# RWKV pairs: three engines' instructions held in the order of the source, projections fed in stated numbers, weight loads issued five blocks ahead

## The chip, the core and the metric

The kernel runs on one core of a Trainium2 chip. The time is the device time of one execution, in microseconds. Five engines work beside each other, each through its own queue and in that queue's order: TensorE (PE; PEld is its weight load), VectorE (DVE), ScalarE (ACT), GpSimd (POOL) and SyncE (SP), the last of which here only issues DMAs. An instruction that waits on another engine's result holds up what stands behind it on its own.

## What is computed

A decoder block for 512 tokens of width 2048: RWKV-7 time mixing and windowed attention beside each other, both read from one projection of the normed input, merged by two sigmoid gates, then a gated convolutional FFN. The change lies in the RWKV part and in the projections that run beside it:

```python
h = rms_norm(x, norm1_g[l])
z = h @ w_in[l]                      # r, k, v, LoRA inputs, attention, gates
zs = token_shift(z[..., :RW_SHIFT_COLS], rw_mu[l])
...
def step(state, inp):                # 512 steps, 16 heads of 64
    r_t, k_t, v_t, w_t, ka_t, kb_t = inp
    sa = jnp.einsum('bhvk,bhk->bhv', state, ka_t)
    state = (state * w_t[:, :, None, :] + sa[..., None] * kb_t[:, :, None, :]
             + v_t[..., None] * k_t[:, :, None, :])
    y = jnp.einsum('bhvk,bhk->bhv', state, r_t)
    return state, y
...
y = ((y - mu) * lax.rsqrt(var + GN_EPS)).reshape(B, S, RW_DIM)
out = (y + bonus.reshape(B, S, RW_DIM)) * g.astype(f32)
```

## The kernel before

**Projections.** A tile of z is 128 channels by 512 tokens and is summed over 2048 inputs in 16 steps of 128. Weights and input are float32, each split into a high part and a remainder, and each step is three matmuls of 128x512: high by high, high by remainder, remainder by high (L255, L256, L257). So a tile is 48 matmuls. Its weights come in four blocks of four steps: a DMA of 256 KB into a tile `raw` (SP's queue), the high part `whi` copied by ScalarE (L238), the remainder `wlo` subtracted by VectorE (L239), and twelve matmuls. There are four buffers each of raw, whi and wlo.

**Pairs.** The 16 heads are worked in eight pairs, a pair being 128 channels. The recurrence is turned into chunks of 64 tokens, eight of them. `early(p)` makes a pair's rows: the k, r and v tiles with their token shift (`zpad` on ScalarE, then `kz`, `rz`, `vz` on VectorE, L536 and L537), k's norm (`rsqrt_small`, thirteen small steps on `rq` tiles, then a trip through DRAM that spreads it over rows), the decay (`lw`, two scans `Ei`, two exponentials into `Et` and `Ei`), and the bonus `bon`. `late(p)` makes the products of a chunk: grams `OW` and `AM` of `BKK` and `BAR`; a triangular inverse that is doubled from blocks of one to blocks of 64; the decayed keys `KD` and `KO`; and the chain.

**Levels.** The loop over `LEVELS[1:]` has five rounds. Each makes a first product `AI` by X (L773, L774: 16 short matmuls on float16 halves), sums and masks it on VectorE (L776, L790), splits it into `IW` (L791, L792), makes a second product `BT` by IW, sums that, writes it into `BX` and into X (L794 to L798), and turns X on TensorE (L802) into the next round's `BT` (four copies, L806 on VectorE and L808 on ScalarE). Every round waits for the one before.

**Chain.** The eight chunks follow each other: G from the state SS (L814, L816), U from BX and G (L820, a copy to `UU`), the next SS from KD and U (L827, L828). `final(p)` then adds up the outputs, norms them (square, `ssy`, thirteen `rq` steps, `yd`), turns them back, and multiplies by the gate's LoRA.

**Order.** The program issues late(p), early(p+1), final(p) and three gate tiles for each pair. A scheduler orders each engine's instructions anew: by its own view of what is ready, with program order as priority. Only what goes through `pin` (`tc.keep_in_program_order`) keeps its place: some matmuls (L625, L719, L820) and the splits that ask for it. So in each pair the 288 matmuls of six projections (k, r, v of the next pair and three gates) are laid by the scheduler between the pair's own short work. The output's splits `rhi`, `rlo` and the gates that are left follow the pairs.

Of the kernel before, what the change touches and what calls it, by code (L numbers as in the profile page):

```python
# [18 lines left out]
P = 128  # L19
S = 512  # L20
# [109 lines left out]
def block_kernel(ctx: ExitStack, tc: tile.TileContext, d: Dims, a: dict, out: bass.AP):  # L130
# [66 lines left out]
    def free(ins):  # L197
        return ins

# [76 lines left out]
    if True:  # L276
# [243 lines left out]
        with ExitStack() as pr:  # L520
# [4 lines left out]
            blk = pr.enter_context(tc.tile_pool(name="blk_ps", bufs=3, space=PSUM, reuse_waits="tile"))  # L525
            chn = pr.enter_context(tc.tile_pool(name="chn_ps", bufs=2, space=PSUM, reuse_waits="tile"))
# [95 lines left out]
            def heads_mm(dst, l, r, start, stop):  # L622
                for h, (lo, hi) in reversed(list(enumerate(HV))):
                    w = l[lo:hi] if l.shape[-1] == C else l[lo:hi, lo:hi]
                    pin(pe.matmul(dst[lo:hi], w, r[lo:hi], start=start, stop=stop, skip_group_check=True))  # L625

            def bulk_mm(dst, l, r):
                ps = bulk()
                for n in reversed(range(NCH)):
                    heads_mm(r3(ps)[:, n], l(n), r(n), True, True)  # L630
                act.activation(dst, r3(ps), AF.Copy)

            def early(p):
                wl = lp.tile([P, 2 + NG, P], F32, name="wl", tag="wl", bufs=2)
                sync.dma_start(wl, a["lora"][p].rearrange("p (k c) -> p k c", c=P))
                w2a2 = lora_parts(wl, 0)

                acc = ztile(d.c_k + p * P)
                kz = wtile("kz")
                shifted(acc, PR["mu"] + NP + p, kz, 0)  # L640
                kk = wtile("kk")
                dve.tensor_scalar(kk, kz, col("k_k", p), None, op0=ALU.mult)
                sq = wtile("lg")
                act.activation(sq, kk, AF.Square)
                ps = bulk()
                head_stats(ps, sq)
                rs = rsqrt_small(wk, ps[:, 0 : 2 * NT], None, None, mx=1e-24)
                rb = head_rows(wk, bulk(), rs, "lg")
                dve.tensor_tensor(kk, kk, rb, op=ALU.mult)


                ps = bulk()
                lora(ps, w2a2, (0,), 0)
                lg = wtile("lw")
                act.activation(lg, ps, AF.Tanh, scale=0.5)
                dve.tensor_scalar(lg, lg, 1.0, None, op0=ALU.add)
                Ei = wtile("Ei")
                for hs in (slice(0, S // 2), slice(S // 2, S)):
                    dve.tensor_tensor_scan(Ei[:, hs], going, lg[:, hs], 0.0, op0=ALU.mult, op1=ALU.add)
                act.activation(Et[:, :, 1:], r3(Ei), AF.Exp, scale=-0.5 * SQE)  # L660
                act.activation(Ei, Ei, AF.Exp, scale=0.5 * SQE)

                ps = bulk()
                lora(ps, w2a2, (1,), 0)
                ta = wtile("lw")
                act.activation(ta, ps, AF.Tanh, scale=0.5, bias=half[:, 0, p : p + 1])

                acc = ztile(d.c_r + p * P)
                rz = wtile("rz")
                shifted(acc, PR["mu"] + p, rz, 1)  # L670
                acc = ztile(d.c_v + p * P)
                vz = wtile("vz", 2)
                shifted(acc, PR["mu"] + 2 * NP + p, vz, 0)

                k2 = wtile("k2")
                dve.tensor_scalar(k2, ta, half[:, 1, p : p + 1], half[:, 2, p : p + 1], op0=ALU.mult, op1=ALU.add)
                dve.tensor_tensor(k2, k2, kz, op=ALU.mult)
                dve.tensor_scalar(ta, ta, 0.5, 0.5, op0=ALU.mult, op1=ALU.add)
                kb = kz
                dve.tensor_tensor(kb, kk, ta, op=ALU.mult)  # L680
                rk = wtile("lw")
                dve.scalar_tensor_tensor(rk, rz, col("r_k", p), k2, op0=ALU.mult, op1=ALU.mult)
                ps = bulk()
                pe.matmul(ps, K["bo"], rk, start=True, stop=True)
                bon = wtile("bon", 2)
                dve.tensor_tensor(bon, vz, ps, op=ALU.mult)
                act.activation(bon, bon, AF.Identity, bias=col("gn_b", p))
                return wl, Ei, kk, kb, k2, rz, vz, bon

            def late(p, st):  # L690
                wl, Ei, kk, kb, k2, rz, vz, bon = st
                Eex, Ein = Et[:, :, 0:C], Et[:, :, 1:]
                kb3, k23, Ei3, kk3, rz3, vz3 = (r3(x) for x in (kb, k2, Ei, kk, rz, vz))
                dve.tensor_tensor(BKK[:, :, 0:C], kb3, Ei3, op=ALU.mult)
                dve.tensor_tensor(BKK[:, :, C:P], k23, Ei3, op=ALU.mult)
                for h, hs in enumerate(slice(*x) for x in HV):
                    dve.scalar_tensor_tensor(BAR[hs, :, 1 + h], kk3[hs], -1.0, Eex[hs], op0=ALU.mult, op1=ALU.mult)
# [765 lines left out]
```

## Time and profile before

| what | value |
|---|---|
| three runs | 2847.71, 2839.99, 2846.57 us; median 2846.57 us |
| profiled execution | 2842.14 us, its span 2839.8 us |
| granted TensorE clock, mean | 0.997 |
| RWKV pairs, first gram to the last pair's end | 332.4 to 1100.8 us |
| a steady pair (630.5 to 729.3) | 98.8 us |

Times below are from the profiled execution. A row of a group names line, engine, operation, output and inputs, shape and count, then busy time in us, the mean of one in ns, and the idle time of the engine just ahead with what ended it. A row of a window gives the busy time of each engine within it.

### The profile page before, as it was taken

Reading aid. Unit: us, or ns where it says so; the run is one execution under the profiler, and the core shown is the slowest. Engines: PE = TensorE matmul, PEld = TensorE weight load, DVE = VectorE, ACT = ScalarE, POOL = GpSimd, SP = SyncE. Lnnn points to the kernel's source line nnn. Section 1 sums busy time; section 2 is a strip of 40 time slices with the busy share of each in tenths; the row PEclk is TensorE's granted clock in tenths of the full one; section 3 lists DMA queues with packets and bytes.
Section 4 is the critical chain, followed back from the end, with each engine's and each line's share of the span. In section 5 each row is a group of like instructions: output and inputs, shape, how many; then the busy total and the mean of one; then the engine's idle time right before and its main releaser. Section 6 shows DMA issues by size and latency. Waiting matters only on the chain.

```text
span 2839.8 us, 48133 instructions
## 1 busy us (share of the span) xinstructions
PE 2772.6 (98%) x18722; PEld 2413.2 (85%) x18722; DVE 1975.7 (70%) x3312; ACT 1289.0 (45%) x2075; POOL 230.8 (8%) x307
## 2 busy tenths in 40 slices
PE   7999999999999999999999999999999999999999
PEld 6888777777777777788888999999999999788887
DVE  5566677778777774455668777777777778655555
ACT  5345344334433433322465555555555555444444
POOL 0101000000000001011000101010101110000000
PEclk9999999999999999999999999999999999999999
DMA  6865676676667668888777789888988897877775
GB/s 190 232 155 152 174 181 166 159 179 162 164 152 177 164 173 240 241 245 275 245 260 200 220 237 245 225 226 232 244 229 224 231 241 227 313 242 241 257 257 189
DMA packets 223860, 608.06 MB, mean 214 GB/s; under 512 B 24576, under 2 KB 44688, under 8 KB 222608
## 3 DMA queue, kind: packets, MB, share of 16 engines
q1 hardware_dynamic: 156096, 432.49, 47.4%
q0 software_dynamic: 36832, 134.24, 24.6%
q10 hardware_dynamic: 30704, 38.27, 3.9%
q8 instruction: 146, 2.39, 0.3%
q14 instruction: 82, 0.67, 0.1%
HBM read 554.23 MB, written 174.40 MB: 257 GB/s over the span
## 4 chain that ended last, share of the span: by engine, by line
PE 86%; DVE 8%; DMA 2%; issue 1%; ACT 1%; ACTq 0%; SPq 0%; DVEq 0%
PE X L1164 18%; PE X L1031 11%; PE acc L255 9%; PE acc L257 9%; PE acc L256 9%; PE Y L1031 9%; PE Y L1164 8%; PE Z L1164 4%; PE bulk L625 1%; PE bulk L773 1%; DMA raw<-in_w_z_dram 1%; PE mi L508 1%; DMA raw<-in_w_dn_dram 1%; DVE BT L741 1%; PE bulk L802 1%
## 5 line engine op out<-in xcount | busy, mean ns | idle before, releaser
L257 PE MATMUL acc<-xhi,wlo 128*128 128x512 f32 x1120 | 450.3, 402 | 6.8 <-DVE wlo L239 6.8
L255 PE MATMUL acc<-xhi,whi 128*128 128x512 f32 x1120 | 450.1, 402 | 2.4 <-ACT whi L238 2.4
L256 PE MATMUL acc<-xlo,whi 128*128 128x512 f32 x1120 | 449.1, 401 | 0.0
L238 ACT ACTIVATE whi<-raw 128x512 fp32r<-128x512 f32 x352 | 220.7, 630 | 466.7 <-PE acc L256 353.3
L1024 DVE TENSOR_TENSOR wlo<-raw,whi 128x1024 fp32r<-128x1024 f32 x210 | 257.1, 1225 | 205.9 <-ACT whi L1023 204.3
L239 DVE TENSOR_TENSOR wlo<-raw,whi 128x512 fp32r<-128x512 f32 x352 | 240.3, 688 | 183.2 <-ACT whi L238 177.3
L1023 ACT ACTIVATE whi<-raw 128x1024 fp32r<-128x1024 f32 x210 | 222.6, 1060 | 291.0 <-PE X L1031 154.2
L1164 PE MATMUL X<-b,whi 128*128 128x256 f32 x1472 | 269.2, 283 | 2.3 <-DVE u L1184 0.9
L1147 DVE TENSOR_TENSOR wlo<-raw,whi 128x1024 fp32r<-128x1024 f32 x176 | 215.1, 1223 | 76.8 <-ACT whi L1146 76.5
L1164 PE MATMUL X<-t,whi 128*128 128x256 f32 x1408 | 259.1, 284 | 8.8 <-DVE u L1184 8.3
L1164 PE MATMUL Y<-t,whi 128*128 128x256 f32 x1408 | 257.1, 283 | 0.0
L257 PEld LDWEIGHTS acc<-xhi,wlo 128*128 128x128 f32 x1120 | 211.6, 189 | 46.4 <-DVE wlo L239 10.7
L255 PEld LDWEIGHTS acc<-xhi,whi 128*128 128x128 f32 x1120 | 211.4, 189 | 40.2 <-ACT whi L238 2.8
L256 PEld LDWEIGHTS acc<-xlo,whi 128*128 128x128 f32 x1120 | 211.8, 189 | 36.0
L1146 ACT ACTIVATE whi<-a 128x1024 fp32r<-128x1024 f32 x132 | 139.4, 1056 | 214.7 <-DVE a L1140 213.3
L1164 PEld LDWEIGHTS X<-b,whi 128*128 128x128 f32 x1472 | 229.5, 192 | 3.1 <-issue 2.4
L1164 PEld LDWEIGHTS X<-t,whi 128*128 128x128 f32 x1408 | 221.0, 193 | 9.3 <-DVE u L1184 5.7
L1164 PEld LDWEIGHTS Y<-t,whi 128*128 128x128 f32 x1408 | 219.6, 192 | 0.0
L1164 PE MATMUL X<-b,wlo 128*128 128x256 f32 x736 | 208.4, 283 | 2.1 <-DVE wlo L1147 2.1
L1147 DVE TENSOR_TENSOR wlo<-a,whi 128x1024 fp32r<-128x1024 f32 x132 | 161.7, 1226 | 67.4 <-ACT whi L1146 66.7
L1164 PE MATMUL X<-t,wlo 128*128 128x256 f32 x704 | 200.1, 284 | 0.0
L1164 PE MATMUL Y<-t,wlo 128*128 128x256 f32 x704 | 199.2, 283 | 0.0
(680 smaller groups left out, 5870.3 us busy)
## 6 DMA issues: line engine op xcount, KB each, us to landing
raw<-in_w_up_dram SPq DMA_DIRECT2D x180, 512.0 KB
raw<-in_w_z_dram SPq DMA_DIRECT2D x288, 256.0 KB
s_dn<-in_w_dn_dram POOLq DMA_DIRECT2D x88, 512.0 KB, 6.5
raw<-in_w_up_dram POOLq DMA_DIRECT2D x88, 512.0 KB, 8.3
raw<-s_dn SPq DMA_DIRECT2D x88, 512.0 KB
raw<-in_w_dn_dram SPq DMA_DIRECT2D x66, 512.0 KB
a<-in_w_up_dram SPq DMA_DIRECT2D x48, 512.0 KB
s_dn<-in_w_dn_dram SPq DMA_DIRECT2D x44, 512.0 KB
```

The source lines that it names most:

```text
L238: pin(act.activation(hi, raw, AF.Copy))
L239: pin(dve.tensor_tensor(lo, raw, hi.bitcast(F32), op=ALU.subtract))
L255: pe.matmul(acc, whi[:, j], xhi[:, k], start=first, stop=False)
L256: pe.matmul(acc, whi[:, j], xlo[:, k], start=False, stop=False)
L257: pe.matmul(acc, wlo[:, j], xhi[:, k], start=False, stop=last)
L508: pe.matmul(ps[:, h], pT[:, kb, h], vt[:, n - 1 + kb, g * HD : (g + 1) * HD], start=kb == kbs[0], stop=kb == kbs[-1])
L1023: act.activation(whi, wr, AF.Copy)
L1024: dve.tensor_tensor(wlo, wr, whi.bitcast(F32), op=ALU.subtract)
L1031: pe.matmul(dst, l[:, q, ts], r[:, es], start=fst and j == 0, stop=lst and j == 2, skip_group_check=True)
L1146: pin(act.activation(hi, t, AF.Copy))
L1147: pin(dve.tensor_tensor(lo, t, hi.bitcast(F32), op=ALU.subtract))
L1164: pin(pe.matmul(ps, l[:, k], r[:, k], start=start and k + i == 0, stop=last and i == 2, skip_group_check=True))
```

## The change

Every instruction that TensorE, VectorE or ScalarE gets in the pairs goes through a wrapper that pins it, so that on each engine the program's order is kept (all these instructions carry the wrapper's line, L207). DMAs are not pinned.

```diff
+    class Held:
+        def __init__(self, engine):
+            self.engine = engine
+        def __getattr__(self, name):
+            f = getattr(self.engine, name)
+            return f if name.startswith("dma") else lambda *args, **kw: pin(f(*args, **kw))
...
-            blk = pr.enter_context(tc.tile_pool(name="blk_ps", bufs=3, space=PSUM, reuse_waits="tile"))
-            chn = pr.enter_context(tc.tile_pool(name="chn_ps", bufs=2, space=PSUM, reuse_waits="tile"))
+            blk = pr.enter_context(tc.tile_pool(name="blk_ps", bufs=4, space=PSUM, reuse_waits="tile"))
+            chn = pr.enter_context(tc.tile_pool(name="chn_ps", bufs=1, space=PSUM, reuse_waits="tile"))
```

The projections become a stream of jobs. `feed(n)` issues the next n of its matmuls. Ahead of block n, loads up to block n+4 are issued and splits up to block n+2; the number of buffers stays four.

```diff
+            class Stream:
+                AHEAD, LOADS = 2, 5
...
+                def ready(self, n):
+                    while self.loaded < min(n + self.LOADS, len(self.blocks)):
...
+                        wp["last"] = sync.dma_start(raw.rearrange("p (k c) -> p k c", c=P), b[0])
...
+                    self.parts(n)
+                def parts(self, n):
+                    while self.parted < min(n + self.AHEAD + 1, self.loaded):
...
+                        split(hi, lo, b[1])
...
+                def feed(self, n):
+                    self.split = False
+                    while n and self.jobs:
+                        if next(self.jobs[0], True):
+                            self.jobs.pop(0)
+                        else:
+                            n -= 1
```

`early` and `late` are cut into steps (classes `Early`, `Pair`) which the loop over pairs calls one by one. The sum of a product's two halves, one reduce on VectorE before (L776), is a copy on ScalarE and an add on VectorE; BX is written by ScalarE except in the last round.

```diff
-                    dve.reduce_sum(t, p4.rearrange("p n e c -> p n c e"), axis=AX.X)
+                    act.activation(t, p4[:, :, 1], AF.Copy)
+                    dve.tensor_tensor(t, t, p4[:, :, 0], op=ALU.add)
...
-            st = early(0)
             for p in range(NP):
-                lt = late(p, st)
-                if p + 1 < NP:
-                    st = early(p + 1)
-                final(p, lt)
-                for _ in range(GATES_PER_PAIR * NK // 16):
-                    emit_gate()
+                own = nxt.jobs() if nxt else []
+                for job in [add_gate] + own[:2] + [add_gate] + own[2:] + [add_gate] * (1 if own else 4):
+                    job()
+                do = Pair(st)
+                st.dense_r()
+                if gone:
+                    gone.output_norms()
+                feed(13)
+                g = do.gram(0)
...
+                feed(15)
+                for m in LEVELS[1:]:
...
+                    do.first_out(p4, m)
+                    if i == 1:
+                        do.start_rest()
+                        if gone:
+                            gone.gated()
+                    if i == 2:
+                        do.decayed()
+                    if nxt and i == 3:
+                        nxt.norms()
...
+                    feed((20, 17, 17, 15, 15)[i - 1])
+                    p4 = do.second(m)
...
+                    do.second_out(p4, m)
+                    if i == 1 and nxt:
+                        nxt.k_rows()
+                    if i == 2:
+                        do.centred()
+                    if i == 3:
+                        do.keys_out(pk)
...
+                    feed((11, 12, 10, 10, 12)[i - 1])
+                    if i < 5:
+                        tp = do.turned()
+                along = iter(nxt.along() if nxt else ())
+                for _ in do.chain():
+                    if not stream.split:
+                        step = next(along, None)
+                        if step:
+                            step()
+                    feed(3)
...
+                do.outputs()
+                feed(5)
+                gone, st = do, nxt
+                nxt = Early(p + 2) if p + 2 < NP else None
+            gone.output_norms()
+            gone.scaled()
+            feed(30)
+            gone.back()
+            gone.back_out()
+            feed(12)
+            gone.gate()
+            gone.gated()
+            while gates:
+                add_gate()
+            feed(10 ** 6)
```

The numbers of one pair are 13, 12, 11, 17, 10, 15 (together 78) ahead of the rounds, 84 and 55 in them, 22 times 3 in the chain, and 5: 288, six projections. All gates that are left are issued straight behind the pairs, and the output's splits come after them.

Three places of the orders, before and after. First ScalarE in the rounds, second pair. Before, the copies of the decayed keys stand ahead of the rounds (`lg` is the square of the next pair's k):

```order
L238 ACTIVATE whi<-raw 128x512 x2
L762 ACTIVATE KD<-bulk 64x4x64
L763 ACTIVATE KO<-bulk 64x256
...
L536 ACTIVATE zpad_2830<-acc,par 128x512
L238 ACTIVATE whi<-raw 128x512
L631 ACTIVATE KV<-bulk 128x512
L644 ACTIVATE lg<-kk 128x512
L631 ACTIVATE GV<-bulk 128x512
L238 ACTIVATE whi<-raw 128x512
L794 ACTIVATE BX<-half__4790 64x8x16x2
L797 ACTIVATE XIW<-half__4790 128x128x2
L808 ACTIVATE BT<-bulk 64x8x64 x2
```

After, in the third and fourth round:

```order
L207 ACTIVATE half__5171<-bulk 128x8x32
L207 ACTIVATE XIW<-half__5171 128x32x8
L207 ACTIVATE BX<-half__5171 64x8x4x8 x2
L207 ACTIVATE KD<-bulk 64x4x64
L207 ACTIVATE KO<-bulk 64x256
...
L207 ACTIVATE whi<-raw 128x512
L207 ACTIVATE BT<-bulk 64x8x64 x2
L207 ACTIVATE half__5243<-bulk 128x8x32
```

KD and KO alternate four times each in both. They moved from ahead of the first round to the place between the third round's X and the fourth round's BT.

Second, VectorE between two pairs. Before, a split of the running projection stands among the small steps of the output's norm:

```order
L846 TENSOR_REDUCE ssy<-gn 128x8
...
L190 TENSOR_TENSOR rq_5467<-rq_5466 128x8
L191 TENSOR_TENSOR rq_5467<-rq_5467,rq_5465 128x8
L239 TENSOR_TENSOR wlo<-raw,whi 128x512
L192 SCALAR_TENSOR_TENSOR rq_5466<-rq_5467,rq_5466 128x8
...
L851 TENSOR_TENSOR yd<-yt,rq_5466 64x4x64 x4
L239 TENSOR_TENSOR wlo<-raw,whi 128x512
```

After:

```order
L207 TENSOR_TENSOR BAR<-rz,Et 128x8x64
L207 TENSOR_REDUCE ssy<-gn 128x8
...
L207 TENSOR_TENSOR rq_6860<-rq_6860,rq_6858 128x8
L207 SCALAR_TENSOR_TENSOR rq_6859<-rq_6860,rq_6859 128x8
L207 TENSOR_TENSOR wlo<-raw,whi 128x512 x4
L207 TENSOR_TENSOR OW<-bulk,cst 64x4x2x64
```

The splits moved behind all thirteen steps, and the first four of the next pair's blocks stand together.

Third, VectorE in the chain, around the scans of the next pair's decay. Before:

```order
L659 SCALAR_TENSOR_TENSOR Ei<-going,lw 128x256
L825 SCALAR_TENSOR_TENSOR KV<-SS,ee,KV 128x64
L816 TENSOR_TENSOR G<-GV,psG 128x64
L239 TENSOR_TENSOR wlo<-raw,whi 128x512
L676 TENSOR_SCALAR k_5400<-lw,half 128x512
L828 TENSOR_TENSOR SS<-KV,psS 128x64
```

After:

```order
L207 SCALAR_TENSOR_TENSOR Ei<-going,lw 128x256
L207 SCALAR_TENSOR_TENSOR KV<-SS,ee,KV 128x64
L207 SCALAR_TENSOR_TENSOR Ei<-going,lw 128x256
L207 TENSOR_TENSOR wlo<-raw,whi 128x512
L207 TENSOR_TENSOR SS<-KV,link 128x64
L207 TENSOR_TENSOR G<-GV,link 128x64
```

Ahead of this wlo, its whi stands on ScalarE behind both exponentials and the tanh that the second scan releases; the link's SS stands behind that wlo.

More of the change, by code (lines that the diff above doesn't have):

```diff
@@ L624, in heads_mm @@
                     w = l[lo:hi] if l.shape[-1] == C else l[lo:hi, lo:hi]
[L625 to L688, printed above, removed]
@@ new lines, in decayed, with keys @@
+                def decayed(self):
+                    dve.tensor_tensor(BKK, BKK, self.st.ee.unsqueeze(2).to_broadcast([P, NCH, P]), op=ALU.mult)
+                def keys(self):
+                    self.KO = KO = wk.tile([P, NCH, C], F32, name="KO", tag="ko")
+                    pss = []
+                    for g in range(2):
+                        ps = bulk().rearrange("p (n c) -> p n c", c=P)
+                        pss.append(ps)
+                        for j in range(HN):
+                            pe.transpose(ps[:, j], BKK[:, g * HN + j], ident)
+                    return pss
@@ L770, in mm3, with inputs_out @@
+                def inputs_out(self, out):
+                    for dst, ps in zip((self.GV, KV), out):
+                        act.activation(dst, r3(ps), AF.Copy)
+                def mm3(self, wt, both, high):
                     ps = bulk()
@@ new lines, in back, with back_out @@
+                def back(self):
+                    self.pb = bulk()
+                    for t in range(NT):
+                        pe.transpose(self.pb[:, t * P : (t + 1) * P], self.yd[:, t].rearrange("p h c -> p (h c)"), ident)
+                def back_out(self):
+                    self.yc = wtile("gn")
+                    dve.scalar_tensor_tensor(self.yc, self.pb, col("gn_w", self.st.p), self.st.bon, op0=ALU.mult, op1=ALU.add)
+                    self.g2 = lora_parts(self.st.wl, 2)
@@ new lines, in gate, with gated @@
+                def gate(self):
+                    self.pg = bulk()
+                    lora(self.pg, self.g2, tuple(range(NG)), 2)
+                def gated(self):
+                    dve.tensor_tensor(self.yc, self.yc, self.pg, op=ALU.mult)
+                    pool.dma_start(o_rw_d[self.st.p], self.yc)
+            st = Early(0)
+            st.fetch()
+            st.w2a2 = lora_parts(st.wl, 0)
+            for job in st.jobs():
+                job()
+            feed(NK * 3)
+            st.k_rows()
@@ new lines, in block_kernel @@
+            st.stats()
+            st.norms()
+            feed(NK)
+            st.rows()
+            st.decay()
+            feed(2 * NK)
+            st.r_rows()
+            feed(3 * NK)
+            st.v_rows()
+            for step in st.along():
+                if step != st.v_rows:
+                    step()
+            free_engines = pe, act, dve
+            pe, act, dve = (Held(x) for x in free_engines)
+            st.dense_a()
+            gone = None
+            nxt = Early(1)
@@ L873, in block_kernel @@
+            gone.output_norms()
+            gone.scaled()
+            feed(30)
+            gone.back()
+            gone.back_out()
+            feed(12)
+            gone.gate()
+            gone.gated()
+            while gates:
+                add_gate()
+            feed(10 ** 6)
+            pe, act, dve = free_engines
         xbs = ExitStack()
```

501 lines of the change are left out of this document (357 added, 144 removed).

## The prediction

> **What bounds the kernel now.** I read first the profile's page (span, busy time, the chain that ended last), then the windows of the RWKV stage, then TensorE's waits there.
>
> ```profile
> span 2839.8 us, 48133 instructions
> ...
> PE 2772.6 (98%) x18722; PEld 2413.2 (85%) x18722; DVE 1975.7 (70%) x3312; ACT 1289.0 (45%) x2075; POOL 230.8 (8%) x307
> ...
> PE 86%; DVE 8%; DMA 2%; issue 1%; ACT 1%; ACTq 0%; SPq 0%; DVEq 0%
> ```
>
> TensorE is busy for 98% of the span and carries 86% of the chain. The change touches the RWKV pairs only, so the windows there are what counts (columns: PE, PEld, DVE, ACT, POOL busy with counts, clock, DMA share, GB/s):
>
> ```profile
> 630.50:729.30 98.80, 96.07 (x758) 75.08 (x757) 74.60 (x168) 39.55 (x81) 7.09 (x9) 1.00 0.69 167
> 1026.10:1100.80 74.70, 72.41 (x650) 55.79 (x649) 52.24 (x107) 29.48 (x62) 5.68 (x7) 1.00 0.69 173
> 1200.00:1250.00 50.00, 50.00 (x222) 41.40 (x221) 24.02 (x42) 11.68 (x20) 5.93 (x8) 1.00 0.84 251
> ```
>
> The first is one steady pair: 98.8 us, of which TensorE misses 2.7. The second is the last pair, which misses 2.3. The third is projections alone: 50.0 / 222 = 0.225 us a matmul. What TensorE waits for in the six pairs from 432.2 to 1026.1 (total, times, longest):
>
> ```profile
> PE bulk L758 <- DVE BKK L742: 6.1, 6, 1.0
> PE acc L257 <- DVE wlo L239: 5.1, 6, 0.8
> PE bulk L855 <- DVE yd L851: 2.7, 6, 0.5
> ```
>
> Three waits of at most 1.0 us a pair. So all that a better order can win inside eight pairs is about 7 x 2.7 + 2.3 = 21 us, plus what an interruption of the projections costs:
>
> ```profile
> 557.13 0.20 PE L773 MATMUL bulk<-XIW,BT 128*128 128x64 f16 x1
> ...
> 557.58 0.48 PE L255 MATMUL acc<-xhi,whi 128*128 128x512 f32 x1
> 557.90 0.39 PE L256 MATMUL acc<-xlo,whi 128*128 128x512 f32 x1
> ```
>
> A level's product takes 557.58 - 557.13 = 0.45 us, and the first projection after it stands 0.32 before the next, not 0.225: an interruption costs 0.1. The stage has 324 of them before and 305 after, 19 fewer: -2 us, 0.2 a pair. The other matmuls are the same.
>
> **What the change adds: waits in a fixed order.** Before, VectorE and ScalarE took whatever the scheduler thought ready; now each stands behind what the source puts ahead. I walked one pair down the three orders, with these durations (x count | busy, mean ns):
>
> ```profile
> L239 DVE TENSOR_TENSOR wlo<-raw,whi 128x512 fp32r<-128x512 f32 x144 | 98.4, 687 | 49.3 <-ACT whi L238 49.0
> L238 ACT ACTIVATE whi<-raw 128x512 fp32r<-128x512 f32 x145 | 91.4, 631 | 187.7 <-PE acc L256 175.5 <-DMA raw<-in_w_z_dram 7.6 <-PE bulk L625 3.7
> L808 ACT ACTIVATE BT<-bulk 64x512 f16<-64x512 f16 x48 | 28.4, 592 | 27.1 <-DVE BT L806 26.5
> L806 DVE COPY BT<-bulk 64x512 f16<-64x512 f16 x48 | 20.1, 420 | 10.4 <-PE bulk L802 6.7 <-ACT BT L808 1.3
> ...
> L752 DVE TENSOR_TENSOR VV<-bulk,vm 64x256 f32<-64x256 f32 x24 | 10.1, 420 | 0.2
> L851 DVE TENSOR_TENSOR yd<-yt,rq 64x256 f32<-64x256 f32 x24 | 10.1, 419 | 0.4
> L763 ACT ACTIVATE KO<-bulk 64x256 f32<-64x256 f32 x24 | 9.1, 381 | 0.3
> L762 ACT ACTIVATE KD<-bulk 64x256 f32<-64x256 f32 x24 | 9.0, 377 | 6.3 <-PE bulk L758 6.1
> L742 DVE TENSOR_TENSOR BKK<-BKK,ee 128x1024 f32<-128x1024 f32 x6 | 7.3, 1225 | 0.2
> L192 DVE SCALAR_TENSOR_TENSOR rq<-rq,rq 128x8 f32<-128x8 f32 x36 | 5.9, 165 | 0.8
> L537 DVE SCALAR_TENSOR_TENSOR kz<-acc,omu,zpad 128x512 f32<-128x512 f32 x6 | 4.5, 751 | 0.2
> L642 DVE TENSOR_SCALAR kk<-kz,par 128x512 f32<-128x512 f32 x6 | 2.9, 480 | 0.0
> ```
>
> Operations on a 128x512 tile without a row of their own here I take at 0.69 on VectorE and 0.63 on ScalarE, as wlo and whi. The steps of a level's product (start, duration):
>
> ```profile
> 555.87 0.42 DVE L790 TENSOR_TENSOR half__5887<-half__5887,cst 128x256 f32<-128x256 f32 x1
> 556.32 0.29 DVE L791 CAST XIW<-half__5887 128x256 f16<-128x256 f32 x1
> 556.65 0.42 DVE L792 TENSOR_TENSOR XIW<-half__5887,XIW 128x256 f16<-128x256 f32 x1
> ...
> 558.91 0.42 ACT L794 ACTIVATE BX<-half__5909 64x256 f32<-64x256 f32 x1
> 559.23 0.40 ACT L797 ACTIVATE XIW<-half__5909 128x256 f16<-128x256 f32 x1
> ...
> 559.66 0.43 DVE L798 SCALAR_TENSOR_TENSOR XIW<-half__5909,XIW 128x256 f16<-128x256 f32 x1
> ```
>
> A handover on VectorE costs 0.03 (555.87 + 0.42 to 556.32). The new sum of two halves is a ScalarE copy and a VectorE add, in place of a reduce. The copy has no row: not below 0.40 (L797, the same size), not above 0.59 (L808, twice the size); I take 0.40. At 0.59 four copies a pair add 0.8, some 6 us in all. TensorE's other work between the levels:
>
> ```profile
> L802 PE MATMUL bulk<-id,XIW 128*128 128x128 f16 x192 | 19.1, 222 | 0.1
> ...
> L758 PE MATMUL bulk<-ident,BKK 128*128 128x128 f32 x48 | 6.4, 276 | 6.1 <-DVE BKK L742 6.1
> L369 PE MATMUL bulk<-cst,lg 128*128 128x2 f32 x48 | 6.2, 251 | 0.0
> ```
>
> Per set that is 19.1 / 24 = 0.80 for X turned, 6.4 / 6 = 1.06 for the keys, half of that (0.53) for the values, 6.2 / 6 = 1.03 for k's sums.
>
> *From a level's second product to the next.* It needs the new BT, then IW. Each copy of BT on ScalarE waits for VectorE's copy (L808's idle 26.5), so the two engines run in series.
> - Level 1 to 2: the gated output 0.69, two wlo 1.37, add 0.42, X high 0.40 and low 0.43, kz 0.75, kk 0.48, its square 0.63, whi 0.63, wlo 0.69, copy 0.42, BT 2 x 0.59, half 0.40, then add, mask, cast, subtract 1.55; with handovers 10.2. TensorE has 11 + 17 matmuls, 6.30, and 0.53 + 0.80 + 2 x 0.45: 8.5. **Wait 1.7.**
> - 2 to 3: BKK 1.23, wlo 0.69, add, X 1.25, means 0.86, VV 4 x 0.42, wlo 0.69, and 3.55 from the copy to the end: 10.1. TensorE: 29 matmuls 6.53, k's sums 1.03, 1.70: 9.3. **0.8.**
> - 3 to 4: the 13 steps of k's norm (13 x 0.165 with handovers 2.5), wlo 0.69, add 0.42, X high 0.40, BX 2 x 0.42, then all eight copies of KD and KO (3.0), which now stand ahead of whi and BT, whi 0.63, wlo 0.69, 3.55, the small rows 0.3: 13.0. TensorE: 25 matmuls 5.63, keys 1.06, 1.70: 8.5 with the rows. **4.5, of which 4.1 in one piece.**
> - 4 to 5: rz 0.75, the LoRA weights' split 0.82, wlo, add, X, whi, wlo and 3.55: 8.4 against 25 matmuls and 1.70, 7.3. **1.0.**
>
> *Chain.* ScalarE runs both exponentials and the tanh (3 x 0.63), then whi; VectorE's wlo stands ahead of the link's SS: 3.2 against two feeds of three matmuls, 1.35. **1.9.** The same with zpad, whi, wlo ahead of G: 2.0 against 0.7. **1.3.**
>
> *Pair boundary.* A pair's 288 numbered matmuls are just its six projections, so at its end no split is ready. VectorE must do BAR's r part 0.69, ssy 0.69, 13 small steps 2.5, then wlo 0.69: 4.6 until the third projection, which TensorE reaches after seven matmuls, 1.7. **2.9.** BAR's r part runs beside ScalarE's square.
>
> That is 8.0 + 3.2 + 2.9 = 14.1 a pair, for the 2.7 and 0.2 that go: **+11.2**. Pair 0 has no boundary: +8.3. Pair 7 has no next pair to prepare: 2.9, then 10.1 against 8.2 (2 to 3) and 10.3 against 8.4 (3 to 4): 6.7 - 2.3 - 0.2 = +4.2. Pairs: 6 x 11.2 + 12.5 = **+79.7**.
>
> *Start.* Ahead of the first pair 864 projections end first, then the rest of pair 0's preparation runs without any:
>
> ```profile
> 323.00:333.50 10.50, 10.50 (x57) 8.17 (x55) 8.36 (x13) 3.11 (x5) 0.81 (x1) 1.00 0.77 191
> ```
>
> Before, TensorE is busy there throughout. Now it idles over zpad, vz, six products and the bonus's factors, 5.9 less 0.7 of LoRA matmuls, then over bonus, three parts of BAR and wlo, 3.0: **+8.2**.
>
> *Tail.*
>
> ```profile
> PE acc L255 <- ACT whi L238: 2.4, 1, 2.4
> ```
>
> After pair 7 the stated 30 and 12 find no job, and 48 x 4 gate matmuls come behind. TensorE waits for square, ssy, norm and yd (0.63 + 0.69 + 2.5 + 4 x 0.42, less five matmuls 1.1): 4.4; for gn, the LoRA split and the gated product 1.8; and, the splits of the output now standing behind the last gate's tanh, 2.8 before the next stage. Less the 2.4 and 0.5 that stood here: **+6.1**.
>
> *Loads* I cost at nothing: ScalarE waits for raw 7.6 us in six pairs (L238's row). The fifth block ahead needs a fifth buffer and there are four, so a load waits for a split as before; twice that wait would be 1.3 a pair on ScalarE. k's norm goes through DRAM on SP's queue at level 4 and is read in the chain, behind some 60 fed matmuls (14 us), and the LoRA weights are fetched a level ahead of their split: hidden; without that cover each would be a wait like those on raw, 7.6 us in all six pairs.
>
> *Clock* (same columns as the windows above):
>
> ```profile
> 21.00:24.40 3.40, 1.64 (x11) 0.97 (x11) 3.23 (x12) 3.21 (x9) 0.00 (x0) 1.00 0.01 1
> 24.40:27.80 3.40, 3.40 (x18) 3.40 (x18) 3.40 (x8) 3.32 (x4) 0.00 (x0) 0.50 0.61 178
> 546.60:550.00 3.40, 1.79 (x12) 1.35 (x12) 3.31 (x6) 2.33 (x7) 0.00 (x0) 1.00 0.00 0
> ```
>
> A stretch with TensorE 1.64 busy is followed by 3.4 us at half clock, which lose 1.7; one with 1.79 kept it. The 4.1 us waits of seven pairs cross that line; the next wait (1.0) takes back part: 7 x 0.7, and 1.7 each at start and tail: **+8**.
> The Trainium skill, "TensorE: Matmul & The Clock Gate", section "HAM oscillation — how this bites in real kernels", sets the line at a gap above 3.4 us, and finds a loop with such a gap in each round cold in every round. By that rule too the 4.1 counts, and the sum stays +8; were it to come out below 3.4, only start and tail would count, +3.4, and 2939. The 546.60 row, with 1.6 idle, agrees with it; the 21.00 row, with 1.8 idle in its window, is stricter.
>
> **Sum**, against the profiled execution (2842.1 us, 2.3 more than its span and 4.4 below the median of the three runs): 79.7 + 8.2 + 6.1 + 8 = 102: **2944 us**.
>
> **Rivals.**
> - *Half the waits* (0.16). The walk takes every step in series; where VectorE is further ahead than I have it, say k's norm done before the third level's product, 2.5 goes from the 4.5. Half of all: 2842 + 51 = 2893.
> - *The order covers everything* (0.11), the other side. One mechanism: the fed matmuls outlast the level chains. It decides at level 4, where 13.0 must come below 8.5; VectorE at 75% and ScalarE at 40% of a pair have the room. Then -21 - 2, with start and tail +14: 2833; with those covered too, 2819.
> - *Much of it covered, boundary left* (0.08): 2833 and 7 x 2.9 less half the tail, within a few us of 2842. This is also what comes out if the order changes little.
> - *The clock falls at shorter waits too* (0.05): the boundary's 2.9 and the 1.7, 14 stretches at 1.7: 2944 + 24 = 2968.
>
> **How the numbers follow.** My forecast holds 0.60 with a range of its own of 2905 to 2975 (the copy at 0.59 and a microsecond a pair either way). The range is 2866 to 2975: it takes in half the waits and the clock, and leaves out the two cases near or below 2842 (0.19). A measurement tells 0.3%, about 8.5 us: faster 0.11, same 0.08, slower 0.81.
>
> **What would show it.** A steady pair of about 110 us in place of 98.8, its TensorE busy time unchanged near 96. Waits for XIW in each level, the longest at level 4 behind BT, with ScalarE's KD and KO ahead of it; waits for wlo at each pair's start behind rq; TensorE idle some 8 us ahead of the first gram; half clock behind level 4. If pairs stay under 100 us with waits below 1 us, the walk is wrong: then the chains overlap where I put them in series.

## The result and the profile after

The changed kernel takes 2946.93 us (median of four runs, 2945.11 to 2952.44), the kernel before 2847.06 (four runs beside them). The ratio is 1.0364, 95% interval 1.0349 to 1.0378: **3.6% slower**. The profiled execution took 2945.25 us. The page of the changed kernel:

```profile
span 2943.5 us, 48021 instructions
...
PE 2797.9 (95%) x18722; PEld 2447.1 (83%) x18722; DVE 1940.9 (66%) x3272; ACT 1331.7 (45%) x2195; POOL 229.8 (8%) x307
...
PE 82%; DVE 8%; ACT 5%; issue 2%; DMA 2%; ACTq 0%; DVEq 0%; SPq 0%; POOLq 0%
```

TensorE has 25 us more busy time for the same 18722 instructions, and ScalarE, 1% of the chain before, is 5% of it. Where the 103.7 us of span came from, by stretches cut at the same instructions in both traces (first gram of a pair, last output product, first `rhi` matmul):

| stretch | before | after | projections in it | lost |
|---|---|---|---|---|
| ahead of the first gram, from 262 us | 70.4 | 84.1 | 294, 307 | 10.8 |
| pairs 0 to 6 | 693.7 | 768.0 | 2016, 2016 | 74.3 |
| last pair | 74.6 | 93.3 | 208, 270 | 4.7 |
| tail to the first `rhi` | 67.3 | 64.1 | 272, 197 | 13.7 |
| all else | 1933.9 | 1934.0 | | 0.1 |

Where the two kernels have other numbers of projections in a stretch, 0.225 us for each was taken off. Windows of the changed kernel: a steady pair, the tail, and the stretch ahead of the first gram (PE, PEld, DVE, ACT, POOL busy, clock, DMA share, GB/s):

```profile
894.70:1004.80 110.10, 98.93 (x758) 79.11 (x757) 70.44 (x163) 44.91 (x95) 7.08 (x9) 0.95 0.58 149
...
1207.00:1271.10 64.10, 52.73 (x212) 41.37 (x208) 19.57 (x42) 17.05 (x31) 10.83 (x16) 0.89 0.81 252
320.00:345.70 25.70, 18.43 (x65) 12.90 (x63) 11.92 (x19) 5.30 (x11) 0.80 (x1) 0.80 0.37 103
```

The pair has the same 758 matmuls as before. It is 11.3 us longer than the 98.8 of before: 8.5 us more without a matmul (11.2 for 2.7), and 2.9 us more of busy time at a clock of 0.95. What TensorE waits for in all pairs (total, times, longest):

```profile
PE bulk L207 <- DVE XIW L207: 41.2, 20, 3.4
PE acc L207 <- ACT whi L207: 14.9, 8, 2.2
PE link L207 <- DVE SS L207: 11.8, 7, 1.7
PE link L207 <- DVE G L207: 7.4, 8, 1.4
PE bulk L207 <- ACT KO L207: 7.0, 7, 1.0
PE acc L207 <- DVE wlo L207: 3.7, 7, 0.6
```

The waits for BKK and yd of before are gone; six others stand in their place. One pair, from its start at 673.6 us, wait by wait (start, duration, idle before with its releaser):

```profile
708.51 0.59 PE L207 MATMUL bulk<-XIW,BT 128*128 128x64 f16 x16 [1.56 <-DVE XIW L207]
724.87 0.27 PE L207 MATMUL bulk<-ident,rq 128*8 128x128 f32 x1 [0.98 <-ACT KO L207]
731.93 0.59 PE L207 MATMUL bulk<-XIW,BT 128*128 128x64 f16 x16 [3.32 <-DVE XIW L207]
740.20 0.59 PE L207 MATMUL bulk<-XIW,BT 128*128 128x64 f16 x16 [0.87 <-DVE XIW L207]
...
753.40 0.43 PE L207 MATMUL link<-SS,BAR 128*128 128x64 f32 x2 [1.68 <-DVE SS L207]
759.91 0.43 PE L207 MATMUL link<-G,BX 128*128 128x64 f32 x2 [1.00 <-DVE G L207]
779.37 0.50 PE L207 MATMUL acc<-xhi,whi 128*128 128x512 f32 x1 [1.82 <-ACT whi L207]
780.63 0.50 PE L207 MATMUL acc<-xhi,wlo 128*128 128x512 f32 x1 [0.52 <-DVE wlo L207]
```

The first, third and fourth are the second products of levels 2, 4 and 5, then come the chain and the pair's end. The wait of 0.98 is new to the argument: it ends with a KO copy, so the small rows seem to wait for a PSUM bank that the keys still hold (`banks_back` below bears on it). What stands ahead of level 4's BT on ScalarE (four of its rows):

```profile
723.27 0.38 ACT L207 ACTIVATE KD<-bulk 64x256 f32<-64x256 f32 x1
...
726.01 0.38 ACT L207 ACTIVATE KO<-bulk 64x256 f32<-64x256 f32 x1
726.42 0.63 ACT L207 ACTIVATE whi<-raw 128x512 fp32r<-128x512 f32 x1
728.41 1.21 ACT L207 ACTIVATE BT<-bulk 64x512 f16<-64x512 f16 x2 [1.36 <-DVE BT L207]
```

X was turned by 723.3 us, and BT is copied from 728.4 on: eight copies and a split stand between. Level 3 shows no wait at all. The windows around its predecessor say why:

```profile
706.25:709.66 3.41, 1.85 (x27) 1.42 (x25) 3.28 (x7) 1.27 (x3) 0.84 (x1) 1.00 0.42 163
709.66:713.07 3.41, 3.41 (x10) 2.82 (x11) 2.83 (x8) 1.77 (x4) 0.00 (x0) 0.50 0.92 130
```

Behind the 1.56 us wait of level 2 the clock falls to half for one window. TensorE then needs longer for the same matmuls, and the operands of level 3 come in time. In pair 0, where the clock stayed up behind level 2, level 3 waits 0.89 us. The pair shown is one of seven: level 5's wait of 0.87 stands in it alone, because only here the clock stayed up behind the 3.32 us wait of level 4. The start and the tail:

```profile
336.35 2.05 PE L812 MATMUL bulk<-lw,cst 128*128 128x512 f32 x2 [5.11 <-DVE lw L808]
340.56 0.79 PE L207 MATMUL acc<-xhi,whi 128*128 128x512 f32 x1 [2.16 <-ACT whi L207]
...
1212.86 1.09 PE L207 MATMUL bulk<-ident,yd 128*128 128x128 f32 x4 [4.38 <-DVE yd L207]
...
1250.03 0.79 PE L207 MATMUL acc<-xhi,whi 128*128 128x512 f32 x1 [4.38 <-ACT whi L207]
```

The last of these is ScalarE's whi waiting in its turn for a load:

```profile
1249.35 0.63 ACT L207 ACTIVATE whi<-raw 128x512 fp32r<-128x512 f32 x1 [8.50 <-DMA raw<-in_w_z_dram]
```

### The profile page after: what moved, and what is told of

It reads as the page before. It is cut to its first block, busy times and chain, and to the rows that moved or that the text cites. A ratio compares the mean times of both kernels' runs of the same rounds, so it can differ in the third digit from the quotient of the medians.

```text
span 2943.5 us, 48021 instructions
## 1 busy us (share of the span) xinstructions
PE 2797.9 (95%) x18722; PEld 2447.1 (83%) x18722; DVE 1940.9 (66%) x3272; ACT 1331.7 (45%) x2195; POOL 229.8 (8%) x307
## 4 chain that ended last, share of the span: by engine, by line
PE 82%; DVE 8%; ACT 5%; issue 2%; DMA 2%; ACTq 0%; DVEq 0%; SPq 0%; POOLq 0%
PE X L1509 17%; PE acc L207 13%; PE X L1376 11%; PE Y L1376 8%; PE Y L1509 8%; PE bulk L207 4%; PE Z L1509 4%; PE acc L265 4%; PE acc L264 4%; PE acc L266 4%; DVE wlo L207 1%; DVE BT L207 1%; PE acc L680 1%; PE link L207 1%; ACT whi L207 1%
## 5 line engine op out<-in xcount | busy, mean ns | idle before, releaser
L207 PE MATMUL acc<-xhi,whi 128*128 128x512 f32 x832 | 343.9, 413 | 19.3 <-ACT whi L207 19.3
L207 PE MATMUL acc<-xlo,whi 128*128 128x512 f32 x832 | 357.6, 430 | 0.0
L1368 ACT ACTIVATE whi<-raw 128x1024 fp32r<-128x1024 f32 x210 | 222.6, 1060 | 290.1 <-PE X L1376 153.9
L207 PE MATMUL acc<-xhi,wlo 128*128 128x512 f32 x832 | 340.3, 409 | 4.3 <-DVE wlo L207 4.2
L207 DVE TENSOR_TENSOR wlo<-raw,whi 128x512 fp32r<-128x512 f32 x208 | 138.4, 688 | 136.7 <-ACT whi L207 135.4
L207 PEld LDWEIGHTS acc<-xhi,whi 128*128 128x128 f32 x832 | 163.9, 197 | 57.7 <-ACT whi L207 24.3
L207 PEld LDWEIGHTS acc<-xhi,wlo 128*128 128x128 f32 x832 | 163.3, 196 | 37.4 <-DVE wlo L207 9.0
L1491 ACT ACTIVATE whi<-raw 128x1024 fp32r<-128x1024 f32 x176 | 184.4, 1049 | 18.8 <-ACT whi L1491 14.9
L207 PEld LDWEIGHTS acc<-xlo,whi 128*128 128x128 f32 x832 | 163.8, 197 | 29.8 <-issue 1.7
```

The costliest lines, as they stand in the source:

```text
L207: return f if name.startswith("dma") else lambda *args, **kw: pin(f(*args, **kw))
L1368: act.activation(whi, wr, AF.Copy)
L1491: pin(act.activation(hi, t, AF.Copy))
```

## The experiments

The theory: TensorE's work and order are sound, and it is the places of single instructions in the held orders of ScalarE and VectorE, and an empty stream at three points, that make it wait. Each edit is to the changed kernel (span 2943.5 us, profiled run 2945.25); a time without a number of runs is one execution. The part behind the first `rhi`, in which most of these edits change nothing, took from 1671 to 1679 us in these traces, so a few us of the whole time say little and the stretches say more. "Pair" is the time from a pair's first gram to the next one's; in the changed kernel 108.2 to 111.3 us.

**KD and KO behind BT.**

```diff
-                    if i == 3:
-                        do.keys_out(pk)
...
+                    if i == 4:
+                        do.keys_out(pk)
-                    if nxt and i == 4:
+                    if nxt and i == 5:
                         nxt.rows()
```

> Edit of the changed kernel: the eight ScalarE copies of KD and KO stand behind the fourth round's BT and half copy instead of ahead of its whi and BT, and the small rows of k's norm one round later. Theory (the place in ScalarE's order is the wait): the wait for XIW at level 4 falls from 3.3 us to about 1.3, the 1.0 us wait of the small rows for a PSUM bank goes, level 5's wait stays near 0.9: 3 us less in each of eight pairs, 2946 to about 2922. Rival (the wait is VectorE's thirteen norm steps or the new copy-and-add sum, not KD and KO): level 4 still waits over 3 us, and the time stays within 5 us of 2946.

2934.56 us, pairs of 106.4 to 109.5. Its waits at levels 4 and 5:

```profile
722.53 0.59 PE L207 MATMUL bulk<-XIW,BT 128*128 128x64 f16 x16 [1.18 <-DVE XIW L207]
725.85 0.86 PE L207 MATMUL bulk<-id,XIW 128*128 128x128 f16 x8 [0.35 <-ACT XIW L207]
732.37 0.59 PE L207 MATMUL bulk<-XIW,BT 128*128 128x64 f16 x16 [1.67 <-DVE XIW L207]
```

Level 4 waits 1.18 for 3.32 and the wait for the bank is gone, as the theory has it; the rival is out. But level 5 now waits 0.35 + 1.67 for 0.87: the copies moved into the next level's way. The pair gains 2.0 of 4.3 there, pairs 0 to 6 gain 13.7 and the run 11 us, not 24.

**The stream carried over the pair's end.**

```diff
-                for job in [add_gate] + own[:2] + [add_gate] + own[2:] + [add_gate] * (1 if own else 4):
+                for job in ([] if p else [add_gate]) + own[:2] + [add_gate] + own[2:] + [add_gate] * (1 if own else 4):
...
+                if p + 1 < NP:
+                    add_gate()
                 along = iter(nxt.along() if nxt else ())
```

> Edit of the changed kernel: the next pair's first gate joins the stream ahead of the chain, so that blocks of it are split before the pair ends; no feed number changes. Theory (an empty stream is the boundary's wait): the 1.8 and 0.5 us of TensorE idle behind the last five matmuls go to under 0.3, and so does the half-clock stretch behind them (1.5 us): 3.5 us less at each of seven boundaries, about 2922. Rival (VectorE's output norm of 4.6 us is due there whatever the stream holds): the wait comes back within the next blocks, at wlo or at yd, and the time stays within 5 us of 2946.

2917.38 us. One of its pairs:

```profile
659.80:765.50 105.70, 96.06 (x756) 77.38 (x755) 70.39 (x164) 44.89 (x96) 7.12 (x9) 0.98 0.63 155
```

Four of seven pairs take 105.7 us; the boundary's 1.82 and 0.52 are gone and did not come back. VectorE's output norm hides behind two blocks that are already split. 28 us less for seven boundaries is more than the 2.3 us of idle each (16 in sum). The rest is mostly clock, but not one stretch for each boundary: of the 19 half-clock windows (3.41 us each) in pairs 0 to 6 of the changed kernel only two stand behind a boundary, and here 12 are left, others having gone as the pairs came to lie otherwise.

**A gate beside pair 0's preparation.**

```diff
+            add_gate()
+            feed(NK * 3)
             free_engines = pe, act, dve
```

> Edit of the changed kernel: one gate (48 projections) is issued behind pair 0's preparation, before the orders are held, and is missing from the four behind the pairs. Theory (TensorE has nothing to do while pair 0 is prepared): idle ahead of the first gram falls from 7.3 us to under 1.5 and the 10.2 us at half clock there go: 9 to 12 us less, about 2936. Rival (the preparation is a chain that the projections only lengthen, since their splits share VectorE and ScalarE with it): under 4 us less.

2943.10 us, a total that the rival allows, though the stretch itself does most of what the theory says:

```profile
320.00:347.50 27.50, 25.45 (x108) 19.53 (x106) 13.31 (x22) 7.30 (x13) 1.62 (x2) 1.00 0.62 164
```

Cut as in the table above it is 3.1 us longer with 48 projections more (10.8 us): 7.7 gained where 9 to 12 were expected, clock at 1.00 throughout. TensorE still misses 2.1 us (27.50 less 25.45), for 7.3 before. Pairs 0 to 6 took 4.4 us more than in the changed kernel: 2.6 of it is idle time, within 0.8 us pair by pair, and their half-clock windows fell otherwise. So much a single execution moves by itself, and the total says little here; the stretch does.

**Gates in the tail's stream.**

```diff
+            while gates:
+                add_gate()
             gone.output_norms()
             gone.scaled()
             feed(30)
```

> Edit of the changed kernel: the four gates left join the stream ahead of the last pair's output norm, so that the stated 30 and 12 have jobs. Theory (the tail waits for an empty stream): the 4.4 us wait for yd goes to under 0.5 and the half clock behind it (6.8 us) too: 5 to 8 us less, about 2940. Rival (the tail is bound by its transfers: the other 4.4 us there is a wait for raw, with all DMA engines busy): the wait for raw grows by what the yd wait loses, and the time stays within 3 us of 2946.

2945.86 us. Its tail:

```profile
1210.12 0.50 PE L207 MATMUL acc<-xhi,whi 128*128 128x512 f32 x1 [1.75 <-ACT whi L207]
...
1213.39 0.79 PE L207 MATMUL acc<-xhi,wlo 128*128 128x512 f32 x1 [2.54 <-DVE wlo L207]
```

The yd wait is gone and 1.75 + 2.54 us stand in its place: jobs were there, but none was split, since the stream had run empty at the pair's end. The wait for raw fell to 2.0 us instead of growing. The tail is 4.4 us shorter, the last pair 1.3 longer, and the rest of the program, where nothing changed, 5 us longer with more half-clock time (20.9 us for 11.7). The total is the one that the rival named, but not for its reason, since the wait for raw fell; the theory's jobs did not help either while none of them was split.

**TensorE's order alone.**

```diff
-            pe, act, dve = (Held(x) for x in free_engines)
+            pe = Held(pe)
```

> Edit of the changed kernel: only TensorE's order is held by the source; VectorE's and ScalarE's are the scheduler's again, feed numbers and steps unchanged. Theory (what waits is the fixed order of VectorE and ScalarE, since splits, KD, KO and norm steps stand ahead of what TensorE needs): about half the waits go, pairs of 103 to 106 us, 2890 to 2920. Rival (the feed numbers on TensorE are what is wrong, and any order of the other two meets the same gaps): pairs within 1 us of 110, 2940 to 2952.

2856.03 us, beside 2839.26 for the kernel before on the same chip. A steady pair:

```profile
638.70:737.10 98.40, 93.50 (x756) 76.22 (x755) 69.88 (x163) 45.66 (x96) 7.11 (x9) 1.00 0.69 166
```

The same feed numbers and the same matmuls in the same order give 98.4 us. Against the kernel before beside it the loss is 17 us instead of 100: 83 of them go when the two other engines' order is set free, most of the loss and not half. Pairs 0 to 6 take 693.7 us, as before; what is left lies at the start and in the tail. What goes in the pairs are the waits for whi, wlo, SS, G and the bank, and with them 17 of the 19 half-clock windows. The waits for XIW hardly fall:

```profile
PE bulk L207 <- DVE XIW L992: 36.2, 24, 3.4
```

So TensorE still misses 4.9 us of this pair, more than the 2.7 of before, and what makes up for it is that its matmuls take 93.50 us for 96.07. Which of the two other engines' orders counts for more was not tried. At level 4 ScalarE has put the splits ahead, so that no whi stands between KO and BT:

```profile
686.73 0.38 ACT L942 ACTIVATE KO<-bulk 64x256 f32<-64x256 f32 x1
687.13 1.21 ACT L1024 ACTIVATE BT<-bulk 64x512 f16<-64x512 f16 x2
```

**The reduce again.**

```diff
-                    act.activation(t, p4[:, :, 1], AF.Copy)
-                    dve.tensor_tensor(t, t, p4[:, :, 0], op=ALU.add)
+                    dve.reduce_sum(t, p4.rearrange("p n e c -> p n c e"), axis=AX.X)
```

> Edit of the changed kernel: the sum of a product's two halves is one VectorE reduce again instead of a ScalarE copy and a VectorE add. Theory (position, not the new copy, makes the waits): level waits within 0.4 us of those of the change, 2938 to 2954. Rival (the added ScalarE copies, ten a pair at 0.4 us, are the cost): 15 us or more less.

2968.20 us, pairs of 110.4 to 114.6. Both missed: the copy and add of the change save, 19 us of it in pairs 0 to 6 (787 for 768). Level 2 waits 1.98 and level 4 3.59:

```profile
715.70 0.59 PE L207 MATMUL bulk<-XIW,BT 128*128 128x64 f16 x16 [1.98 <-DVE XIW L207]
...
741.57 0.80 PE L207 MATMUL bulk<-XIW,BT 128*128 128x64 f16 x16 [3.59 <-DVE XIW L207]
```

**Powers apart.** The step of the second scan, both exponentials and the tanh becomes three:

```diff
-                    yield lambda: (self.scan(1), self.powers(), self.rate())
+                    yield lambda: (self.scan(1), self.power_t())
+                    yield self.power_i
+                    yield self.rate
```

> Edit of the changed kernel: the second scan with the first exponential, the second exponential, and the tanh are three steps of the chain instead of one, so that a split can stand between them. Theory (three ScalarE operations in a row ahead of whi hold wlo, and it the link's SS): the 1.7 us wait for SS falls under 0.7, seven pairs have 1 us less each, 2946 to about 2937; the 1.0 us wait for G behind zpad stays. Rival (VectorE's work in the chain is too much for its links in any order): the waits of the chain only move to other links, sum within 0.4 us of 2.7, time unchanged.

2943.93 us.

```profile
748.50 0.43 PE L207 MATMUL link<-SS,BAR 128*128 128x64 f32 x2 [1.14 <-DVE SS L207]
754.14 0.43 PE L207 MATMUL link<-G,BX 128*128 128x64 f32 x2 [1.00 <-DVE G L207]
```

The wait for SS falls by 0.5, half of what was expected, and did not move to another link. The whole time does not tell it from nothing, but pairs 0 to 6 took 761.8 us for 768.0, some 0.9 a pair, while the part behind the first `rhi`, which the edit does not touch, took 5.4 more.

**Loads four blocks ahead.**

```diff
-                AHEAD, LOADS = 2, 5
+                AHEAD, LOADS = 2, 4
```

> Edit of the changed kernel: loads are issued four blocks ahead instead of five. Theory (four buffers set how far ahead a load can run, so the fifth block changes nothing): waits and pairs as in the change, 2940 to 2952. Rival (the loads' issue costs or saves something): 10 us or more either way.

2948.89 us, with the same waits: the fifth block changes nothing that can be seen.

**PSUM banks as before** (`blk_ps` 3, `chn_ps` 2).

> Edit of the changed kernel: the PSUM banks as before, three for the bulk products and two for the chain's links. Theory (a fixed order holds more products at once, and the small rows already wait 1.0 us for a bank): the bulk products wait more, 1 to 3 us a pair at the keys and the rows, links unchanged, 2955 to 2970. Rival (one bank for the links is what makes the chain wait): the chain's 2.7 us fall by half or more, 2930 to 2938.

2945.55 us: both missed.

```profile
724.96 0.59 PE L207 MATMUL bulk<-XIW,AI 128*128 128x64 f16 x16 [1.45 <-ACT KO L207]
726.54 0.27 PE L207 MATMUL bulk<-ident,rq 128*8 128x128 f32 x1 [0.99 <-ACT KO L207]
731.92 0.59 PE L207 MATMUL bulk<-XIW,BT 128*128 128x64 f16 x16 [1.69 <-DVE XIW L207]
```

TensorE waits for a bank 1.5 us longer (1.45 + 0.99 for 0.98), and the wait for XIW behind it is 1.6 us shorter (1.69 for 3.32). Both end with the same row of KD and KO copies, so a second wait in that time is free. The chain's waits did not change: the links do not lack a bank.

**All places at once.** The first version (`refilled`) takes all edits above that helped and, from its rows, moves VectorE's side work (k's rows, decayed keys, means, values, one to a level) into the 1.3 us in which it waits for ScalarE's BT. KD and KO go half at level 3 and half at level 4, KD on ScalarE and KO on VectorE:

```diff
+                            if a == h == 1:
+                                beside()
...
-                feed(17)
+                feed(14)
                 do.start_a()
                 do.start_b()
-                feed(10)
+                do.start_rest()
+                feed(9)
...
-                    feed((20, 17, 17, 15, 15)[i - 1])
+                    feed((18, 16, 16, 15, 16)[i - 1])
...
+                    if i in (3, 4):
+                        do.keys_out(i - 3)
                     if i == 5:
                         do.inputs_out(vin)
                         if nxt:
                             nxt.decay()
+                            nxt.r_rows()
+                            nxt.norms()
+                            nxt.decay_plus()
```

> Edit of the changed kernel, all found places at once: stream carried over the pair's end and into the tail, a gate beside pair 0's preparation, KO copied by VectorE and KD by ScalarE in two halves a level apart, k's norm and r's rows behind the last level, VectorE's other work (k's rows, decayed keys, values) inside each level where it waits for ScalarE's BT, the gated product ahead of the first level's sum, powers as three steps; feed numbers shifted to 13, 12, 11, 14, 9, 13 | 18, 16, 16, 15, 16 | 11, 11, 11, 11, 20 | 22 x 3 | 5. Theory (the waits are only places, and TensorE's own work is 96 us a pair in both kernels): pairs of 97 to 100 us, no idle over 1.5 us ahead of the first gram, 2835 to 2855. Rival (VectorE and ScalarE cannot serve the levels in any fixed order at this rate): pairs of 103 us or more, 2885 or more.

2846.98 us, beside 2839.26 for the kernel before on the same chip; pairs of 96.9 to 98.9, no half clock in any of them. Ahead of the first gram 1.8 us of idle are left, for the 1.5 expected. Four waits are left in each pair: 0.65 at level 2, 0.9 at level 4, 1.4 at level 5, 1.0 for G, and one of 4.5 us ahead of the output. The second version takes these on:

```diff
+                def v_pad(self):
+                    self.va = self.pad(self.va, PR["mu"] + 2 * NP + self.p, 0)
...
-                    feed((18, 16, 16, 15, 16)[i - 1])
+                    feed((18, 18, 16, 18, 19)[i - 1])
...
-                    feed(3)
+                    feed(3 if nxt else 2)
...
-                split(ahi[:, i], alo[:, i], ain[2 * i // NQ][:, i % (NQ // 2)])
+                split(ahi[:, i], alo[:, i], ain[2 * i // NQ][:, i % (NQ // 2)], pin)
```

> The kernel refilled, with the four waits that its trace still shows taken on: KD's copies of a half together and KO's behind them, the LoRA weights' split behind the last level, v's zpad as a step of its own in the chain, two gates at the start, more feed at levels 1, 3, 4 and 5 (18, 18, 16, 18, 19 and 11, 11, 11, 12, 12), two instead of three per link in the last pair, and the attention splits held behind the output's. Theory (each wait left is a place and a number): pairs of 96 to 97.5 us instead of 98.7, no 4.5 us wait ahead of the output's matmuls, 2820 to 2832, 0.4 to 0.9% faster than before. Rival (VectorE is full, so waits move to the next place): pairs stay at 98 to 99 us and the time within 5 us of before.

2815.08 us (four runs), 0.9900 of the kernel before (2841.91, seven runs beside it), 95% interval 0.9883 to 0.9917: 1.0% faster than before, and better than expected. Its steady pair, and all that TensorE waits for from the first gram to the output:

```profile
631.60:726.60 95.00, 94.28 (x756) 76.04 (x755) 72.09 (x168) 43.26 (x92) 7.07 (x9) 1.00 0.70 173
```

```profile
PE bulk L207 <- DVE XIW L207: 3.6, 16, 0.6
PE acc L264 <- ACT rhi L210: 1.8, 1, 1.8
PE link L207 <- DVE SS L207: 1.5, 8, 0.2
PE link L207 <- ACT UU L207: 0.8, 1, 0.8
```

For comparison TensorE's order alone, with the stream carried over and two gates at the start:

> Edit of the changed kernel: only TensorE's order held (as in pe_only), with the stream carried over the pair's end and into the tail and two gates at the start. Theory (with the other two engines' order free, what is left of the loss is the empty stream at start, boundary and tail, 5.6, 2 a pair and 6.7 us of idle): 2830 to 2842. Rival (the scheduler has already laid VectorE's and ScalarE's work into those gaps): time within 4 us of pe_only's 2856.

2826.05 us, 0.9946 of before (0.9931 to 0.9960): the theory, a little better than its range. `refilled2` is 11 us shorter than this, but it also has other feed numbers, KD and KO shared by two engines, and the attention's splits behind the output's. How much of the 11 us comes from holding the two other engines is open: its places with TensorE's order alone held were not run.

## Why the prediction was right

Forecast 2944, measured 2946.93. The sum against the profiled execution was +102; the spans differ by 103.7. The mechanism is shown by the runs: the boundary's wait goes when the stream is carried over it, two thirds of level 4's go when KD and KO move (half of that comes back at level 5), a third of SS's when the powers are apart, and with all places moved together 0.7 us of idle are left in a pair. The tail's waits only moved under `tail_fed`. That the total came within 3 us is luck, as the three rows below show. The terms (a pair's boundary counted with the pair that it ends, as the stretches are cut; the prediction counted it with the next):

| term | forecast | measured |
|---|---|---|
| level 1 to 2 | 1.7 | 1.56 |
| level 2 to 3 | 0.8 | 0, behind a half-clock window |
| level 3 to 4 | 4.5 | 0.98 + 3.32 |
| level 4 to 5 | 1.0 | 0.87 |
| chain, SS and G | 1.9, 1.3 | 1.68, 1.00 |
| pair boundary | 2.9 | 1.82 + 0.52 |
| pairs 0 to 6, with their clock | 78.4 + 5 | 74.3 |
| last pair | 1.3 | 4.7 |
| start, with its clock | 8.2 + 1.7 | 10.8 |
| tail, with its clock | 6.1 + 1.7 | 13.7 |

The same difference by kind, from the two traces:

| kind | forecast | measured |
|---|---|---|
| TensorE idle | 96 | 78 |
| its matmuls at full clock | -2 | -15 |
| half clock | 8 | 40 |

Half clock is counted as half of the time that TensorE is busy in half-clock stretches: 94.5 us in the changed kernel, 14.3 before. In the pair from 894.7, whose TensorE is busy for 98.93 us, these are the stretches:

```profile
931.52:934.94 3.42, 3.42 (x10) 2.63 (x9) 2.83 (x8) 1.76 (x4) 0.00 (x0) 0.50 0.91 163
952.00:958.83 6.83, 5.78 (x33) 4.51 (x34) 4.06 (x9) 2.46 (x6) 0.00 (x0) 0.50 0.53 156
```

Half of 9.2 taken off, 94.3 us are left, which is what the pair of `refilled2` takes at a clock of 1.00 (94.28).

- **The waits** were found at their places and are 17% smaller in sum (11.8 for 14.1 in that pair). The walk took handovers and small steps in series; the boundary's thirteen norm steps cost 0.2 each as assumed, but splits and two ready matmuls ran a little earlier. Over all pairs part of what is missing is the clock's doing: level 3's 0.89 stands in pair 0 alone and level 5's 0.87 in the pair shown alone, since in the others half clock stands ahead of them. That is about 11 of the 17 us.
- **The clock** was the term most mis-sized: I took +8 and it cost 40, of which 31 in pairs 0 to 6, 3 at the start, 5 in the tail and 1 behind it. The fall behind level 4 came in six of seven pairs, as forecast. But it came as well behind the 1.56 us of level 2 in six, behind the 1.68 us for SS in three, and behind two boundaries: what happened is the rival of a clock that falls at shorter waits too, to which I gave 0.05.
- **TensorE's own work** was the other: 19 interruptions fewer at 0.1 were to save 2 us, and the pair was to stay near 96 busy. At full clock it is 94.3, and 93.50 where TensorE's order alone is held. So the held order of TensorE saves about 2 us a pair; what in it does so was not tried.
- So 2944 was hit because idle time 17 us and matmuls 13 us smaller than forecast made up for a clock 32 us dearer. Only some 11 us of that belong together: at half clock TensorE comes later and waits less.
- **The tail** came out 6 us dearer than its term, and the last pair 3 (it waits 2.81 at level 4 and 1.42 for G, for 1.9 and nothing). The yd wait is as forecast (4.38 for 4.4); what was not is the wait for raw, 4.4 where 2.4 stood before, and half clock behind both (5.3 us for 1.7). Why that load is later was not tried; with jobs in the stream earlier it was 2.0.
- **Loads** at nothing: right (loads_four). The **copy and add** was taken as a step of the chain with no thought of its gain; reduce_back shows 19 us of it in the pairs.
- **The rival of covered waits** had its deciding point right: from level 3's second product to level 4's it is 12.8 us in the trace, of which TensorE has work for 8.5 (13.0 and 8.5 in the walk). The room that VectorE and ScalarE have is real: refilled2 uses it. The change's own order does not.

## What to carry to other kernels

Where several engines are held in program order, walk the queue of each between one product that TensorE waits for and the next, with durations from the trace: the sum in series against TensorE's own work there gave six of the seven waits of the pair shown to within 0.6 us. Work that nothing waits for (KD and KO, norm steps, the next tile's rows) belongs into the time in which its engine waits anyway, and a stream of independent matmuls must not run empty where others are about to wait. With such places and the feed numbers moved, the kernel with three held orders went from 3.6% slower than the one with the scheduler's to 1.0% faster. And a total that agrees does not show that its terms do: time them one by one.

## What the runs showed of the hardware

The clock falls at shorter waits than expected. The half-clock stretches of a trace begin on a grid of 3.41 us. Over the fourteen traces of this study, in the RWKV stage from 330 to 1275 us, every window on that grid at full clock was sorted by the time that TensorE is busy in it:

| busy in the window | windows | followed by half clock |
|---|---|---|
| under 1.5 us | 81 | 80 |
| 1.5 to 2.0 us | 171 | 93 |
| 2.0 to 2.6 us | 317 | 12 |

So about half of the window decides, and not one gap's length. The waits of 1.82 and 0.52 at a pair's end (779.37 and 780.63) were enough in the pair shown, where most of both falls into one window (busy 1.44 us), and in pair 0, but not in the five others, where the grid lies otherwise. The 3.32 us wait at 731.93, which the grid cuts in two, lowered nothing. The Trainium skill, "TensorE: Matmul & The Clock Gate", section "HAM oscillation — how this bites in real kernels", has a gap of more than 3.4 us as the line; these rows lie below it, and they decide. The busy time of pipelined matmuls is modelled, so the bound between the rows of the table is not sharp.
